# The state group's output matrices on VectorE, and its recurrence over 64 chunks in two levels of eight

## The chip, the cores and the metric

The kernel runs on one core of one Trainium2 chip. The metric is the device time of one execution in microseconds. The kernel before took 1163.69 us in the median of three runs (1162.95 to 1164.85). Five engines work side by side, each through its own queue in order: TensorE (matrix products, PE in the profile), VectorE (DVE), ScalarE (ACT), GpSimd (POOL) and SyncE (SP, which here only issues transfers). SBUF is the on-chip memory, PSUM holds the results of products.

## The reference

One layer of an encoder with a sequence of 256 and a width of 2048, in float32. The projection `x @ w_in` gives q, k, v for 16 attention heads of 64 and u for a state group of width 1024. The change touches the state group alone: 64 groups of 16 channels drive a 64-dimensional complex diagonal state each.

```python
dt = jnp.exp(log_dt)[:, None]
decay = jnp.exp(dt * a_re)
ab_re = decay * jnp.cos(dt * a_im)
ab_im = decay * jnp.sin(dt * a_im)
...
bu_re = jnp.einsum("blgp,gnp->blgn", uf, bb_re)
bu_im = jnp.einsum("blgp,gnp->blgn", uf, bb_im)
...
_, _, s_re, s_im = lax.associative_scan(_complex_linear_combine, elems, axis=1)
y = (jnp.einsum("blgn,gpn->blgp", s_re, c_re)
     - jnp.einsum("blgn,gpn->blgp", s_im, c_im)
     + d_skip * uf)
```

So s[t] = a s[t-1] + B u[t] with complex a, and y = Re(C s) + D u. Then follow a GELU and a gate (`ssm * sigmoid(ssm @ w_glu + b_glu)`), RMS norms of both groups, `w_out`, a layer norm, a feed-forward part with a depthwise convolution (5632 wide), and a second layer norm.

## The kernel before

**The stream of weights.** All large products run over chunks of weights of 128x1024 floats. `dma_chunk` loads one through SyncE's queue, `split_chunk` makes a high part (ScalarE, line 163) and a low part (VectorE, line 164, called lo) out of it, and three products with the two parts take the place of one in float32. In iteration j of `run`, chunk j + 3 is split, chunk j + 7 is loaded and the products of chunk j are issued. Four buffers each hold the raw, high and low parts. Phase 1 has 104 chunks: v (0 to 7), u (8 to 23), v again (24 to 31), k and q in turn (32 to 63, four chunks for a pair of heads), the attention half of w_out (64 to 79), the gate (80 to 87) and the state half of w_out (88 to 103). Phase 2 is the feed-forward part.

**Side work.** At the end of every iteration each generator in `self.sides` whose start has come is advanced by one step: `s5_params` (from chunk 0), `s5_loc` (16), `s5_cm` (22), `s5_kstack` (24), `s5_scan` (35), and the attention of head pair j (from chunk 36 + 4j). `paced` turns a list of instructions with costs into steps: it issues until the summed costs reach a budget, then yields to the next chunk. Small products that come one by one between the large ones go through `put` and `fill`.

**The order of each engine's queue** is not the order of the program alone. A planner takes all instructions with their dependencies, models the engines, and puts on each engine the ready instruction of the highest priority, which is the earliest in the program where nothing else is set (`high_priority` moves some ahead). It also sets the waits. On the chip each engine runs its queue in that fixed order.

**The state group** is computed by chunks of four time steps, 64 chunks in all.
- `s5_params` computes a, its powers and f B on VectorE (tiles in `prm`), 32 columns wide, and `MB`, the matrices a^s f B (line 682, 128x512).
- `s5_loc` transposes MB on TensorE (lt) and multiplies it with u (ll, line 764), which gives every chunk's own contribution to the state, copied into `X[P, 2, 32, 64]`: real and imaginary part, 32 columns (pairs of groups), 64 chunks. `loc_done` is set when that is done.
- `s5_scan` then runs the recurrence over the chunks, `X[c+1] += a^4 X[c]`: 63 steps one after the other, each with four VectorE instructions of 128x64 (lines 819 to 822), with a cost of 1.0 a step and a budget of 2.5 a chunk of weights. `cA` holds the real part of a^4 twice, `cB` the imaginary part with both signs, so that a complex product with a swapped view of X needs two products and two additions.
- `s5_kstack` and `Kt` hold the direct path of u within a chunk (kernels of lags 0 to 3); `Kt` is set to zero by GpSimd (line 866) and filled by eight transfers.
- `s5_cm` forms the output matrices CM = (Re(C a^i), -Im(C a^i)) in four groups of eight columns, in two halves each. Per half GpSimd does two products of 128x512 into scratch (lines 909 and 910, columns 1024 to 2047 of the tile `kcm`) and two additions of 64x512 into CM (line 914), after two memsets per group (lines 900 and 901). The first group lies in half of the tile named `vtok`; the second and third use the slot of MB, the fourth that of `scb`, so they start when MB and scb are no longer read. The second and fourth also wait for `k_done` and `lt_done`.
- `s5_y` multiplies CM with X and Kt with u (line 940), copies the sums to `ysh` (which takes the slot of `kcm`), applies the GELU and splits the result into `ssmhl` (which takes the slot of X) for the gate.

**The attention** of a pair of heads: `evac_k` and `evac_q` add up kz and qt on VectorE (lines 500 and 505), `scores` is a product (S, line 1012), `soft` and `norm` are the softmax on VectorE and ScalarE (lines 1021 to 1031), `trans` transposes the probabilities on TensorE (T, line 1036), `pv` multiplies with v (O, line 1048). There is one kz pair and one qt for all pairs of heads, and the last step of a pair waits for `cm_ready`.

The lines that set the pace of the recurrence:

```python
V.tensor_tensor(u, s[:, ::-1], self.cB, op=ALU.mult)
V.tensor_tensor(w, s, self.cA, op=ALU.mult)
V.tensor_tensor(u, u, t, op=ALU.add)
V.tensor_tensor(t, w, u, op=ALU.add)
yield from self.paced([(1.0, lambda c=c: step(c)) for c in range(63)], 2.5)
```

Of the kernel before, what the change touches and what calls it, by code (L numbers as in the profile page):

```python
# [20 lines left out]
P = 128  # L21
# [36 lines left out]
def host_layout(x, w_in, attn_rel_bias, ssm_a_re, ssm_a_im, ssm_log_dt, ssm_b_re, ssm_b_im,  # L58
# [25 lines left out]

    # groups by (half, column): pairs as they are, and the order whose transposes are pairs
    col, half = np.arange(NP_)[None, :], np.arange(2)[:, None]
# [32 lines left out]
class Builder:  # L119
# [6 lines left out]

# [1 line left out]
    def fill(self):  # L128
# [8 lines left out]

# [1 line left out]
    def add(self, src, mm, post=None, hold=None):  # L139
# [58 lines left out]

# [1 line left out]
    def mm_a(self, ps, hi, lo, xs, k0, first, last, nk=8):  # L200
# [13 lines left out]
    def mm_f(self, ps, hi, lo, k0, first, last, part=None):  # L214
        """product with x1, whose columns are (token tile, high or low part, token)"""
        nc, xs = self.nc, self.x1
        th = lambda a: a.rearrange("p (t h c) -> p t h c", t=2, h=2)[:, :, 0]
        for kk in range(8):
            x = xs[:, k0 + kk]
            w = slice(kk * P, (kk + 1) * P)  # L220
            start, stop = first and kk == 0, last and kk == 7

            def low():
                nc.tensor.matmul(th(ps), lhsT=lo[:, w], rhs=th(x), start=False, stop=False)  # L224
            if part == 0:
                nc.tensor.matmul(ps[:, 0:SEQ], lhsT=hi[:, w], rhs=x[:, 0:SEQ], start=start, stop=False)
                continue
            c = slice(0, 512) if part is None else slice(SEQ, 512)
            if stop:
                low()  # L230
            nc.tensor.matmul(ps[:, c], lhsT=hi[:, w], rhs=x[:, c], start=start and part is None, stop=stop)  # L231
            if not stop:
                low()
# [23 lines left out]

# [1 line left out]
    def build(self):  # L259
# [30 lines left out]

    # phase 1 -----------------------------------------------------------------
    def plan_phase1(self):
# [83 lines left out]
        add_v(1)  # L376
        # k, q
        for j in range(8):
            for c in range(4):
# [9 lines left out]
                self.add(I["wkq"][4 * j + c], mm, post)  # L389
        # w_out, attention half  # L390
        def wo_attn(nb, c):
# [8 lines left out]
        for nb in (2, 3):  # L400
            for c in range(4):
                wo_attn(nb, c)
        # glu
        for f in range(8):
# [3 lines left out]
            self.add(I["wg"][f], mm, lambda f=f: self.evac_glu(f, cur["ps"]))  # L408
        # w_out, state half; the last two blocks one token tile after the other
        for nb in range(4):  # L410
# [53 lines left out]
    def evac_ab(self, ps, name, scale=None):  # L464
        """second half of a product of the split operands, copied out of PSUM"""
        t = self.t1([P, SEQ], name)
# [39 lines left out]

    # S5 ----------------------------------------------------------------------
    def s5_load(self):
# [40 lines left out]
    def s5_params(self):  # L549
# [46 lines left out]
        exp(dec, dec)  # L596
        # sin and cos by the quadrant of th
        ts(k, th, 0.6366197723675814, MUL, MAGIC, ADD)
# [62 lines left out]
        def cmul(o, ia, a, b, w):  # L661
            # o, a: [P, 2, 4, NP_] tiles at index; (o = a*b)
            (orr, oi), (ar, ai), (br, bi) = o, a, b
# [11 lines left out]
        ts(self.scb[:, 1], self.scb[:, 1], -1.0, MUL)  # L675
        # a^(s) f B, s = 0..3
        MB = self.MB = bp.tile([P, 2, NP_, 4, SG], F32, tag="d0", name="MB")
# [23 lines left out]
        cmul(pa(3), None, pa(1), pa(1), None)  # L701
        cA = self.cA = ap.tile([P, 2, NP_], F32, name="cA")
        cB = self.cB = ap.tile([P, 2, NP_], F32, name="cB")
        ops.append((0.2, lambda: V.tensor_copy(cA[:, 0], PA[:, 0, 3])))
        ops.append((0.2, lambda: V.tensor_copy(cA[:, 1], PA[:, 0, 3])))
        ts(cB[:, 0], PA[:, 1, 3], -1.0, MUL)
        ops.append((0.2, lambda: V.tensor_copy(cB[:, 1], PA[:, 1, 3])))
        # -C_im
        ts(self.sc[:, 1], self.sc[:, 1], -1.0, MUL)
# [3 lines left out]
    def reorder(self, a, o):  # L713
        """values of the groups in the order of the transposes, brought to the order of the pairs"""
        nc = self.nc
# [92 lines left out]

    def s5_scan(self):
        while not self.loc_done:  # L810
            yield
        V, X, ap = self.nc.vector, self.X, self.ap_

        def step(c):
            s = X[:, :, :, c]
            t = X[:, :, :, c + 1]
            u = ap.tile([P, 2, NP_], F32, tag="su", bufs=2, name=f"su{c}")
            w = ap.tile([P, 2, NP_], F32, tag="sw", bufs=2, name=f"sw{c}")
            V.tensor_tensor(u, s[:, ::-1], self.cB, op=ALU.mult)
            V.tensor_tensor(w, s, self.cA, op=ALU.mult)  # L820
            V.tensor_tensor(u, u, t, op=ALU.add)
            V.tensor_tensor(t, w, u, op=ALU.add)
        yield from self.paced([(1.0, lambda c=c: step(c)) for c in range(63)], 2.5)
        for _ in range(2):
            yield
        yield from self.s5_y()

    def s5_kstack(self):
# [39 lines left out]
        for g2 in range(2):  # L868
            for i in range(4):
                # rows s >= 3-i hold the kernel of lag s-(3-i)  # L870
                n = SG * (i + 1)
# [5 lines left out]
    def s5_cm(self):  # L877
        nc, bp, ap = self.nc, self.bp, self.ap_
        Gp = nc.gpsimd
        self.CM = []  # L880
# [5 lines left out]
        for pg in range(4):  # L886
# [20 lines left out]
            for ri in range(2):  # L907
                # C holds (re, -im): re(C a) and -im(C a)
                Gp.tensor_tensor(t0, cr if ri == 0 else ci, ar, op=ALU.mult)
                Gp.tensor_tensor(t1, ci if ri == 0 else cr, ai, op=ALU.mult)  # L910
                for g2 in range(2):
                    r = slice(64 * g2, 64 * g2 + 64)
                    o = self.CM[pg][r, ri].rearrange("p c (e g q) -> p g c e q", g=2, q=SG)[:, g2]
                    Gp.tensor_tensor(o, t0[r], t1[r], op=ALU.add if ri == 0 else ALU.subtract)
                yield
# [36 lines left out]
    def evac_glu(self, f, ps):  # L952
# [7 lines left out]
        nc.vector.tensor_tensor(s, ps[:, 0:SEQ], t, op=ALU.add)  # L960
        # sigmoid(z) = (1 + tanh(z / 2)) / 2; the half is taken at the group's norm
        nc.scalar.activation(s, s, AF.Tanh, bias=self.bh[:, f:f + 1], scale=0.5)
# [35 lines left out]

    # attention -----------------------------------------------------------------
    def attention(self, j):  # L1000
# [85 lines left out]

    # w_out and layer norm 1 ------------------------------------------------------
    def load_x(self):
# [81 lines left out]

    # phase 2 -----------------------------------------------------------------
    def plan_phase2(self):
# [176 lines left out]
```

## Time and profile before

| what | value |
|---|---|
| median of three runs | 1163.69 us (1162.95 to 1164.85) |
| span of the profiled execution, first to last instruction | 1161.2 us |
| TensorE busy | 1120.5 us (96%) |
| VectorE busy | 772.8 us (67%) |
| ScalarE busy | 563.1 us (48%) |
| GpSimd busy | 121.6 us (10%) |
| mean granted TensorE clock | 0.985 |

Times in the profile are microseconds from the first instruction of one profiled execution. That execution is listed by its span alone; what lies around it is seen only in the difference to the runs' median. "Busy" is the time in which an engine has an instruction at work; on VectorE one instruction's record can overlap the next one's, so the distance between the starts of two neighbours is what an instruction costs there when many follow each other. Rows of groups give line, engine, operation, output and inputs, shape, the count, busy time, the mean of one in ns, and the idle time before them with what ended it. PEclk is the granted clock of TensorE, 1.00 being full.

### The profile page before, as it was taken

To read this page: it belongs to the slowest core of one execution; us is meant where nothing else is said; L and a number is where in the kernel's file an instruction comes from. 1 tells how busy PE (TensorE), PEld (TensorE's weight loads), DVE (VectorE), ACT (ScalarE), POOL (GpSimd) and SP (SyncE) were. 2 spreads that over 40 slices of the span, in tenths; PEclk is the share of its full clock that TensorE was granted. 3 is DMA by queue.
4 is the path that set the end of the run, shared out by engine and by line. 5 is a ranking of instruction groups with operands and counts; after the bars stand their busy time and mean duration, and the time that the engine had idled before them with its cause. 6 is when DMAs were issued, how large, how long until landed. Compare 5 with 4: busy or idle time off the path is not lost.

```text
span 1161.2 us, 18034 instructions
## 1 busy us (share of the span) xinstructions
PE 1120.5 (96%) x6936; PEld 946.9 (82%) x6936; DVE 772.8 (67%) x1379; ACT 563.1 (48%) x849; POOL 121.6 (10%) x125
## 2 busy tenths in 40 slices
PE   8999959999999889999999999999999999999996
PEld 6887747887787778888888888888888888888885
DVE  7993399994678866666666666666666545454555
ACT  5454325553666545555555555555555433333350
POOL 2031870000001270000000000000000000000001
PEclk9999979999999989999999999999999999999998
DMA  8786324443666446556656666666665766666661
GB/s 299 281 234 147 104 83 146 155 150 97 225 193 204 150 140 212 183 182 189 190 184 183 194 185 182 185 187 190 185 186 190 258 196 192 193 196 192 190 198 73
DMA packets 63589, 212.04 MB, mean 183 GB/s; under 512 B 7568, under 2 KB 13072, under 8 KB 62864
## 3 DMA queue, kind: packets, MB, share of 16 engines
q1 hardware_dynamic: 62320, 208.38, 57.7%
q0 software_dynamic: 896, 2.10, 0.8%
q8 instruction: 54, 0.88, 0.3%
q10 hardware_dynamic: 288, 0.43, 0.1%
q14 instruction: 31, 0.25, 0.1%
HBM read 207.46 MB, written 3.41 MB: 182 GB/s over the span
## 4 chain that ended last, share of the span: by engine, by line
PE 88%; DVE 7%; DMA 2%; POOL 1%; issue 1%; ACT 1%; SPq 0%; ACTq 0%; POOLq 0%; DVEq 0%
PE f L231 27%; PE f L224 14%; PE d L247 7%; PE d L249 7%; PE d L245 7%; PE kq L209 3%; PE u L209 2%; DVE lo L164 2%; PE kq L211 2%; PE oa L245 1%; PE oa L247 1%; PE u L211 1%; PE oa L249 1%; PE glu L209 1%; PE v L247 1%; PE v L249 1%
## 5 line engine op out<-in xcount | busy, mean ns | idle before, releaser
L164 DVE TENSOR_TENSOR lo<-raw,hi 128x1024 fp32r<-128x1024 f32 (+1 forms) x358 | 441.0, 1233 | 246.0 <-ACT hi L163 242.2
L163 ACT CAST hi<-raw 128x1024 fp32r<-128x1024 f32 (+1 forms) x358 | 374.4, 1046 | 299.8 <-PE d L249 125.9
L231 PE MATMUL f<-x1s,hi 128*128 128x512 f32 (+1 forms) x1408 | 491.2, 398 | 6.4 <-ACT hi L163 4.2
L224 PE MATMUL f<-x1s,lo 128*128 128x256 f32 x1408 | 382.6, 283 | 0.5 <-DVE lo L164 0.5
L231 PEld LDWEIGHTS f<-x1s,hi 128*128 128x128 f32 x1408 | 261.2, 190 | 63.1 <-ACT hi L163 4.5
L224 PEld LDWEIGHTS f<-x1s,lo 128*128 128x128 f32 x1408 | 268.0, 190 | 9.5 <-DVE lo L164 1.0
L247 PE MATMUL d<-lo,hid 128*128 128x512 f32 (+1 forms) x360 | 133.4, 371 | 0.0
L245 PE MATMUL d<-hi,hid 128*128 128x512 f32 (+1 forms) x360 | 133.4, 370 | 0.0
L249 PE MATMUL d<-hi,hid 128*128 128x512 f32 (+1 forms) x360 | 133.3, 370 | 0.0
L209 PE MATMUL kq<-xs,hi 128*128 128x512 f32 x240 | 89.8, 412 | 3.1 <-DVE qt L505 3.1
L1324 POOL TENSOR_TENSOR res<-res,gb 128x416 f32<-128x416 f32 x2 | 2.9, 1444 | 721.6 <-ACT res L1323 721.6
L245 PEld LDWEIGHTS d<-hi,hid 128*128 128x128 f32 x360 | 67.8, 188 | 11.8
L247 PEld LDWEIGHTS d<-lo,hid 128*128 128x128 f32 x360 | 67.8, 188 | 11.6
L249 PEld LDWEIGHTS d<-hi,hid 128*128 128x128 f32 x360 | 67.8, 188 | 11.5
L211 PE MATMUL kq<-xs,lo 128*128 128x256 f32 x240 | 69.2, 288 | 0.0
L209 PEld LDWEIGHTS kq<-xs,hi 128*128 128x128 f32 x240 | 45.6, 190 | 14.5 <-DVE qt L505 3.5
L1279 ACT COPY ga<-f 128x256 f32<-128x256 f32 x44 | 16.4, 374 | 82.4 <-PE f L231 82.4
L1286 DVE TENSOR_TENSOR gp<-f,ga 128x256 f32<-128x256 f32 x44 | 18.7, 425 | 45.0 <-ACT ga L1279 45.0
L1279 ACT COPY va<-f 128x256 f32<-128x256 f32 x44 | 16.3, 371 | 64.7 <-PE f L231 64.7
L1298 DVE TENSOR_TENSOR va<-f,va 128x256 f32<-128x256 f32 x44 | 18.7, 424 | 42.3 <-ACT va L1279 42.3
L211 PEld LDWEIGHTS kq<-xs,lo 128*128 128x128 f32 x240 | 45.8, 191 | 0.9
L209 PE MATMUL u<-xs,hi 128*128 128x512 f32 x120 | 43.5, 401 | 0.0
(214 smaller groups left out, 1418.1 us busy)
## 6 DMA issues: line engine op xcount, KB each, us to landing
raw<-wf SPq DMA_DIRECT2D x176, 512.0 KB, 3.7
raw<-wd SPq DMA_DIRECT2D x88, 512.0 KB, 4.3
raw<-wkq SPq DMA_DIRECT2D x32, 512.0 KB, 3.6
raw<-wo SPq DMA_DIRECT2D x32, 512.0 KB, 3.9
raw<-wu SPq DMA_DIRECT2D x16, 512.0 KB, 4.5
raw<-wv SPq DMA_DIRECT2D x15, 512.0 KB, 6.1
raw<-wg SPq DMA_DIRECT2D x8, 512.0 KB, 4.4
bd<-band SPq DMA_DIRECT2D x16, 128.0 KB, 3.0
```

Of the source, the lines that this page charges most:

```text
L163: self.nc.scalar.copy(hi[:, c], raw[:, c])
L164: self.nc.vector.tensor_tensor(lo[:, c], raw[:, c], hi[:, c].bitcast(F32), op=ALU.subtract)
L209: nc.tensor.matmul(ps, start=first and kk == 0, stop=False, **h)
L211: nc.tensor.matmul(ps[:, 0:SEQ], start=False, stop=False, **l)
L224: nc.tensor.matmul(th(ps), lhsT=lo[:, w], rhs=th(x), start=False, stop=False)
L231: nc.tensor.matmul(ps[:, c], lhsT=hi[:, w], rhs=x[:, c], start=start and part is None, stop=stop)
L245: nc.tensor.matmul(ps, lhsT=ah, rhs=wh, start=first and kk == 0, stop=False)
L247: nc.tensor.matmul(ps, lhsT=ah, rhs=wl, start=False, stop=False)
L249: nc.tensor.matmul(ps, lhsT=al, rhs=wh, start=False, stop=last and kk == 1)
L1279: self.nc.scalar.copy(tv, v[:, :, 1])
L1286: nc.vector.tensor_tensor(g[:, 2:].rearrange("p (t c) -> p t c", t=2), p0, t, op=ALU.add)
L1298: nc.vector.tensor_tensor(tv, p0, tv, op=ALU.add)
```

## The change

1. In `s5_cm` the two products and the two additions of each half are issued on VectorE. The memsets stay on GpSimd.
2. `s5_params` no longer forms cA and cB. It forms QR and QI, the powers 1 to 8 of a^4 (real part twice, imaginary part with both signs), by doubling, with 22 small VectorE instructions. QR lies in columns 512 to 1023 of `kcm`.
3. `s5_scan` views the 64 chunks as 8 blocks of 8. First, within all blocks at once, 7 steps of 512 elements (stepping through X by 8 elements); then 7 steps of 64 elements over the last chunks of the blocks; then, block by block, 7 steps of 448 elements that add the power times the last state of the block before. That is 21 steps of four instructions and not 63. Costs are 2.7, 1.1 and 2.4, the budget 3.0 a chunk. Scratch is in the same columns of `kcm` that `s5_cm` uses, and the two empty steps before `s5_y` are gone.

Comments were also taken out.

```diff
@@ s5_params
-        cA = self.cA = ap.tile([P, 2, NP_], F32, name="cA")
-        cB = self.cB = ap.tile([P, 2, NP_], F32, name="cB")
...
+        QR = self.QR = self.kcm[:, 512:1024].rearrange("p (r c k) -> p r c k", r=2, k=8)
+        QI = self.QI = ap.tile([P, 2, NP_, 8], F32, name="QI")
+        q0, q1 = [self.kcm[:, c:c + 128].rearrange("p (c k) -> p c k", k=4) for c in (1024, 1536)]
+        ops.append((0.2, lambda: V.tensor_copy(QR[:, 0, :, 0], PA[:, 0, 3])))
+        ops.append((0.2, lambda: V.tensor_copy(QI[:, 1, :, 0], PA[:, 1, 3])))
+        for n in (1, 2, 4):
+            br, bi = [q.unsqueeze(2).broadcast_to([P, NP_, n]) for q in (QR[:, 0, :, n - 1], QI[:, 1, :, n - 1])]
+            ar, ai = QR[:, 0, :, 0:n], QI[:, 1, :, 0:n]
...
+            tt(QR[:, 0, :, n:2 * n], s0, s1, SUB)
...
+            tt(QI[:, 1, :, n:2 * n], s0, s1, ADD)
+        ops.append((0.3, lambda: V.tensor_copy(QR[:, 1], QR[:, 0])))
+        ops.append((0.3, lambda: V.tensor_scalar(QI[:, 0], QI[:, 1], -1.0, None, op0=ALU.mult)))
@@ s5_scan
-        def step(c):
...
-        yield from self.paced([(1.0, lambda c=c: step(c)) for c in range(63)], 2.5)
-        for _ in range(2):
-            yield
+        X = self.X.rearrange("p r c (b k) -> p r c b k", k=8)
...
+        def madd(cost, o, s, ar, ai, shape):
+            n = math.prod(shape[1:])
+            def f():
+                u, w = (self.kcm[:, c:c + n].rearrange("p (r x) -> p r x", r=2) for c in (1024, 1536))
...
+                V.tensor_tensor(u, s[:, ::-1], ai, op=ALU.mult)
+                V.tensor_tensor(w, s, ar, op=ALU.mult)
+                V.tensor_tensor(u, u, o, op=ALU.add)
+                V.tensor_tensor(o, w, u, op=ALU.add)
+            ops.append((cost, f))
+        sh = [P, 2, NP_, 8]
+        one = lambda q, k: q[:, :, :, k]
+        for k in range(1, 8):
+            bc = lambda q: one(q, 0).unsqueeze(3).broadcast_to(sh)
+            madd(2.7, X[:, :, :, :, k], X[:, :, :, :, k - 1], bc(QR), bc(QI), sh)
+        for b in range(1, 8):
+            madd(1.1, X[:, :, :, b, 7], X[:, :, :, b - 1, 7], one(QR, 7), one(QI, 7), [P, 2, NP_])
+        sh2 = [P, 2, NP_, 7]
+        for b in range(1, 8):
+            madd(2.4, X[:, :, :, b, 0:7], X[:, :, :, b - 1, 7].unsqueeze(3).broadcast_to(sh2),
+                 QR[:, :, :, 0:7], QI[:, :, :, 0:7], sh2)
+        yield from self.paced(ops, 3.0)
@@ s5_cm
-                Gp.tensor_tensor(t0, cr if ri == 0 else ci, ar, op=ALU.mult)
-                Gp.tensor_tensor(t1, ci if ri == 0 else cr, ai, op=ALU.mult)
+                V.tensor_tensor(t0, cr if ri == 0 else ci, ar, op=ALU.mult)
+                V.tensor_tensor(t1, ci if ri == 0 else cr, ai, op=ALU.mult)
...
-                    Gp.tensor_tensor(o, t0[r], t1[r], op=ALU.add if ri == 0 else ALU.subtract)
+                    V.tensor_tensor(o, t0[r], t1[r], op=ALU.add if ri == 0 else ALU.subtract)
```

More of the change, by code (lines that the diff above doesn't have):

```diff
@@ L701, in s5_params @@
         cmul(pa(3), None, pa(1), pa(1), None)
-        cA = self.cA = ap.tile([P, 2, NP_], F32, name="cA")
-        cB = self.cB = ap.tile([P, 2, NP_], F32, name="cB")
[L704 to L707, printed above, removed]
+        QR = self.QR = self.kcm[:, 512:1024].rearrange("p (r c k) -> p r c k", r=2, k=8)
[6 more added lines that the diff above has]
+            ar, ai = QR[:, 0, :, 0:n], QI[:, 1, :, 0:n]
+            s0, s1 = q0[:, :, 0:n], q1[:, :, 0:n]
+            tt(s0, ar, br, MUL)
+            tt(s1, ai, bi, MUL)
+            tt(QR[:, 0, :, n:2 * n], s0, s1, SUB)
+            tt(s0, ar, bi, MUL)
+            tt(s1, ai, br, MUL)
+            tt(QI[:, 1, :, n:2 * n], s0, s1, ADD)
+        ops.append((0.3, lambda: V.tensor_copy(QR[:, 1], QR[:, 0])))
+        ops.append((0.3, lambda: V.tensor_scalar(QI[:, 0], QI[:, 1], -1.0, None, op0=ALU.mult)))
         ts(self.sc[:, 1], self.sc[:, 1], -1.0, MUL)
@@ L811, in s5_scan @@
             yield
-        V, X, ap = self.nc.vector, self.X, self.ap_
-        def step(c):
[L815 to L822, printed above, removed]
-        yield from self.paced([(1.0, lambda c=c: step(c)) for c in range(63)], 2.5)
-        for _ in range(2):
-            yield
+        V = self.nc.vector
+        X = self.X.rearrange("p r c (b k) -> p r c b k", k=8)
+        QR, QI = self.QR, self.QI
+        ops = []
+        def madd(cost, o, s, ar, ai, shape):
+            n = math.prod(shape[1:])
+            def f():
+                u, w = (self.kcm[:, c:c + n].rearrange("p (r x) -> p r x", r=2) for c in (1024, 1536))
+                if len(shape) == 4:
+                    u, w = (t.rearrange("p r (c k) -> p r c k", k=shape[3]) for t in (u, w))
+                V.tensor_tensor(u, s[:, ::-1], ai, op=ALU.mult)
[15 more added lines that the diff above has]
+        yield from self.paced(ops, 3.0)
         yield from self.s5_y()
@@ L878, in s5_cm @@
         nc, bp, ap = self.nc, self.bp, self.ap_
-        Gp = nc.gpsimd
+        Gp, V = nc.gpsimd, nc.vector
         self.CM = []
```

## The prediction

> **What bounds the kernel now.** I read the page first, then busy time by stretch, then the waits of TensorE, and last the single instructions of the stretch that stood out.
>
> ```profile
> span 1161.2 us, 18034 instructions
> PE 1120.5 (96%) x6936; PEld 946.9 (82%) x6936; DVE 772.8 (67%) x1379; ACT 563.1 (48%) x849; POOL 121.6 (10%) x125
> POOL 2031870000001270000000000000000000000001
> PEclk9999979999999989999999999999999999999998
> ```
>
> TensorE is the bound as a whole. Of GpSimd's 121.6 us most lies in the fourth to sixth slice (29 us each), and the granted clock falls exactly behind it. The next rows cut phase 1 at the places where something changes (columns: stretch, its length, busy time and instructions of PE, PEld, DVE, ACT, POOL, then the clock).
>
> ```profile
> 80.00:114.00 34.00, 33.56 (x366) 26.56 (x365) 12.86 (x14) 16.18 (x23) 8.29 (x12) 1.00 0.68 166
> 114.00:142.60 28.60, 28.60 (x222) 20.98 (x221) 11.18 (x12) 8.62 (x12) 25.40 (x21) 1.00 0.36 112
> 149.70:167.25 17.55, 5.47 (x31) 2.92 (x31) 17.45 (x24) 4.81 (x14) 16.39 (x13) 0.61 0.27 81
> 203.00:259.30 56.30, 56.12 (x322) 46.23 (x324) 55.71 (x230) 30.65 (x72) 2.96 (x4) 1.00 0.48 150
> ```
>
> From 114 to 142.6 TensorE is full while VectorE idles 28.6 - 11.2 = 17.4 us. From 149.7 to 167.25 TensorE works 5.5 of 17.6 us, at a clock of 0.61, and VectorE is full. From 203 to 259 both are full. What TensorE waited for between 143 and 180:
>
> ```profile
> PE T L1036 <- DVE sT L1031: 8.4, 2, 6.3
> PE kq L209 <- DVE qt L505: 3.1, 1, 3.1
> PE O L1048 <- ACT pT L1040: 0.6, 1, 0.6
> ```
>
> That is 12.1 us. Behind the long wait the matmuls also ran slowly for a time:
>
> ```profile
> 157.51 1.11 PE L1048 MATMUL O<-pT,vtok 128*64 128x256 f32 x2 [0.57 <-ACT pT L1040]
> ...
> 170.62 0.44 PE L209 MATMUL kq<-xs,hi 128*128 128x512 f32 x1
> ```
>
> The first takes 1.11 us where the same product later takes 0.58 (quoted below), and at 170.6 the pace is normal again. From 156.0 to 170.6 there are 14.6 - 5.8 (the shorter waits) = 8.8 us of work at half speed, which would take 4.4 less. So at most 12.1 + 4.4 = 16.5 us is to be had here. Why VectorE was late shows in its own times, the first five rows from 146.3 to 167 and the last five the same kinds from 168 to 258.
>
> ```profile
> L164 DVE TENSOR_TENSOR lo<-raw,hi 128x1024 fp32r<-128x1024 f32 x2 | 4.2, 2120 | 0.0
> L819 DVE TENSOR_TENSOR su<-X,cB 128x64 f32<-128x64 f32 x3 | 3.6, 1185 | 0.1
> L822 DVE TENSOR_TENSOR X<-sw,su 128x64 f32<-128x64 f32 x3 | 3.2, 1077 | 0.1
> L1031 DVE TENSOR_SCALAR sT<-sT,mx 128x256 f32<-128x256 f32 x2 | 2.7, 1346 | 0.0
> L1031 DVE TENSOR_SCALAR sT<-sT,mx 128x128 f32<-128x128 f32 x2 | 2.7, 1332 | 0.0
> ...
> L164 DVE TENSOR_TENSOR lo<-raw,hi 128x1024 fp32r<-128x1024 f32 x22 | 27.5, 1249 | 0.0
> L822 DVE TENSOR_TENSOR X<-sw,su 128x64 f32<-128x64 f32 x57 | 15.2, 267 | 0.3
> L819 DVE TENSOR_TENSOR su<-X,cB 128x64 f32<-128x64 f32 x56 | 15.1, 269 | 0.5
> L1031 DVE TENSOR_SCALAR sT<-sT,mx 128x256 f32<-128x256 f32 x11 | 3.8, 347 | 0.0
> L1031 DVE TENSOR_SCALAR sT<-sT,mx 128x128 f32<-128x128 f32 x11 | 3.1, 280 | 0.0
> ```
>
> Each costs 0.8 to 1.05 us more: 2 x 0.87 + 3 x 0.92 + 3 x 0.81 + 2 x 1.00 + 2 x 1.05 = 11.0 us on these twelve. In that time GpSimd forms the output matrices, and the ends fall together:
>
> ```profile
> 151.16 2.08 POOL L910 TENSOR_TENSOR kcm<-prm 128x512 f32<-128x512 f32 x1
> 152.28 0.99 DVE L1022 TENSOR_SCALAR mx<-mx 128x2 f32<-128x2 f32 x1
> ```
>
> A VectorE instruction over two elements ends at 153.27, with GpSimd's (153.24). So the two engines hold each other up, and the stall is VectorE's backlog. By 203 it is gone, and from there TensorE sets the pace.
>
> **The change part by part.** **The output matrices:** 16 instructions of 128x512 and 16 of 64x512 go from GpSimd to VectorE; GpSimd keeps eight memsets and that of Kt. Prices on VectorE come from these rows (instructions of one group follow each other at the distance of their starts):
>
> ```profile
> 71.16 0.68 DVE L682 TENSOR_TENSOR MB<-MB,mbt 128x512 f32<-128x512 f32 x1
> 71.76 0.68 DVE L682 TENSOR_TENSOR MB<-prm 128x512 f32<-128x512 f32 x1
> 76.40 1.25 DVE L563 TENSOR_TENSOR prm<-prm 128x32 f32<-128x32 f32 x11
> 145.86 0.26 DVE L820 TENSOR_TENSOR sw<-X,cA 128x64 f32<-128x64 f32 x1
> 146.04 0.26 DVE L821 TENSOR_TENSOR su<-su,X 128x64 f32<-128x64 f32 x1
> ```
>
> 512 elements in a row cost 0.60, so 32 instructions cost 19.2 us. The first group's eight (4.8 us) can start when the parameters are done near 80, where VectorE idles 21 us up to 114. The other 24 (14.4 us) must wait until the slots of MB and scb come free behind the kernel-stack product:
>
> ```profile
> 109.52 3.92 PE ks L839 x128
> ```
>
> From 113.4 on they fit the 17.4 us that are idle before 142.6. I count them at nothing. The cover is thin: whatever spills past 142.6 is paid, up to 9.6 us for two groups. The gain is that the contention is gone: 11 us of VectorE's time.
>
> **The powers QR, QI:** 22 small instructions for 4 removed, between 0.11 (the 32-element row) and 0.26 us each, 2.4 to 5.7 us, say 3.8, near 80, where the idle time just named follows. Nothing.
>
> **The recurrence:** 63 steps x 4 instructions of 64 elements become 7 x 4 of 512, 7 x 4 of 64 and 7 x 4 of 448. Unmixed, a step takes 0.97 us, from one first instruction to the next:
>
> ```profile
> 143.74 0.26 DVE L819 TENSOR_TENSOR su<-X,cB 128x64 f32<-128x64 f32 x1
> ...
> 144.71 0.27 DVE L819 TENSOR_TENSOR su<-X,cB 128x64 f32<-128x64 f32 x1
> ```
>
> Mixed with other work the gaps between dependent instructions are filled, and it costs 4 x 0.18 = 0.72; I take 0.75. From 168 to 258 VectorE did 57 steps (43 us) and the rest of 22 chunks (rows above: 22 splits), with no idle time, so the rest is (90 - 43) / 22 = **2.15 us a chunk**. The new first level walks X in steps of 8 elements, which no row shows at 512. Lower bound: 0.60 each as in MB, 2.4 us a multiply-add. Upper: 32 elements in a row start 0.107 apart, 512 start 0.60 apart, so 64 in a row would be 0.14, but the strided rows show 0.18; 0.04 over 64 elements is 0.32 over 512, hence 0.92 each, and 4.1 with gaps where an instruction needs the one before. I take three at 0.92 and the last, which only writes strided, at 0.7, with 0.15 of gaps: **3.6 us**, since the recurrence's own walk is the nearest row. Second level: a step as now, 0.75 to 0.97, take 0.80. Third: runs of 7 in a row, 0.53 to 0.6 each, take 2.3. Sum 7 x 3.6 + 7 x 0.8 + 7 x 2.3 = 25.2 + 5.6 + 16.1 = **46.9 us** (37 to 52), against 63 x 0.75 = 47 now. The two levels save VectorE nothing; they only hand the work out faster, over 14 chunks where 25 were used (cost units 2.7, 1.1, 2.4 against a budget of 3.0, and 63 x 1.0 against 2.5).
>
> [...]
>
> **What it does to TensorE:** the recurrence starts at 143.74, with the split of chunk 41 just done. Splits run up to three chunks ahead of the products. The last of the new recurrence is emitted with chunk 52, so ahead of the split of chunk 56. VectorE reaches that split after 15 chunks of other work: 143.7 + 46.9 + 15 x 2.15 = **222.8**. Before, chunk 40 starts behind the last wait:
>
> ```profile
> 167.25 0.79 PE L209 MATMUL kq<-xs,hi 128*128 128x512 f32 x1 [3.07 <-DVE qt L505]
> 207.22 0.58 PE O L1048 x2
> 222.37 0.58 PE O L1048 x2
> ```
>
> Four chunks take 15.15 us (the two rows are the same product of successive head pairs), 3.8 each, so chunk 56 starts at 167.25 + 16 x 3.8 = 228.0. Without any stall TensorE would be there at 228.0 - 16.5 = 211.5, but it can't pass the split. Gain 228.0 - 222.8 = **5.2 us**. From there on TensorE is the bound as before, VectorE has 1.7 us a chunk to spare, and the y products, the same number as now, stand among the kq products and not behind them. Scratch in kcm, and ysh in its slot, add only orders on VectorE itself. The results ysh and ssmhl come earlier than now, so nothing behind them waits longer. The profiled span of 1161.2 becomes 1156.0; the median of 1163.69 lies 2.5 us above the span (start and end outside it), so the forecast is **1158.5**.
>
> [...]
>
> **The rivals.**
> *Clean:* the first level costs near 2.4 us, VectorE then reaches the split at 143.7 + 37 + 32.2 = 212.9, almost where TensorE is; gain 15.1, 1148.6. For it: MB's products read broadcast operands at 0.68. Against it: the strided rows.
> *Even:* the first level costs 4.1 and the rest its upper bounds, 143.7 + 52.3 + 32.2 = 228.2; gain 0, 1163.7.
> *Slower:* TensorE is held by the transposes and not by the splits. It runs in order, and a transpose waits for the softmax, which stands in VectorE's queue among instructions of 0.92 instead of 0.18 us.
>
> ```profile
> 183.41 0.33 PE L1036 MATMUL T<-ident,sT 128*128 128x128 f32 x1 [0.79 <-DVE sT L1031]
> 198.09 0.30 PE L1036 MATMUL T<-ident,sT 128*128 128x128 f32 x1 [0.20 <-DVE sT L1031]
> 203.13 1.21 DVE L164 TENSOR_TENSOR lo<-raw,hi 128x1024 fp32r<-128x1024 f32 x1
> ```
>
> At 203.13 VectorE splits chunk 52 while TensorE, by 3.8 us a chunk, stands in 49.4: the transposes, not the splits, held it 2.6 chunks back. If that lead can't be used up, TensorE is at 53.4 when VectorE reaches 56 at 222.8; before, it was there at 167.25 + 13.4 x 3.8 = 218.2. Loss 4.6 us, 1168.3. It decides from a lead of 1.4 chunks that stays unused. Against it: the order of TensorE's queue is planned anew with the longer instructions, so transposes can stand later.
>
> **How the numbers follow.** Forecast, a gain of 2.3 to 10 us: 0.40. Clean: 0.18. Even, within 2.3 us (0.2%, about what a measurement of this kernel tells from no change): 0.18. Slower: 0.24. So faster 0.58, same 0.18, slower 0.24. The range reaches from the clean case with a little over (1147) to the slower one (1168.5); the forecast's own is 1153 to 1161.
>
> **What would show it.** Right: VectorE's splits stay near 1.25 us and the softmax's scaling near 0.35 from 146 to 167; GpSimd shows no 512-element products; the 6.3 us wait shrinks below 3; VectorE is full from 143 to about 223 and TensorE shows small waits there; y products start near 225, among the kq products. The strided first level shows at 0.9 to 1.0 us an instruction (0.68 if clean). Wrong: output-matrix instructions on VectorE behind 143.7; waits on sT that together pass 16.5 us; a new wait of y for X; a change outside 80 to 300 us.

## The result and the profile after

The changed kernel takes 1171.32 us (median of 4 runs, 1170.06 to 1171.85) against 1164.27 us (1162.95 to 1165.29) for the kernel before on the same chip: a ratio of 1.0061, 95% interval 1.0048 to 1.0073. It is slower by 7 us. The forecast was 1158.5 us. The profiled execution has a span of 1169.5 us against 1161.2.

The head of the page, the kernel after:

```profile
span 1169.5 us, 17878 instructions
PE 1122.2 (96%) x6936; PEld 949.3 (81%) x6936; DVE 788.0 (67%) x1261; ACT 565.8 (48%) x850; POOL 81.0 (7%) x93
POOL 2031100000002180000000000000000000000001
PEclk9999988999999998999999999999999999999998
```

GpSimd's block in the fifth and sixth slice is gone (121.6 us before, 81.0 now) and the dip of the granted clock is less deep, but two slices long (146 to 205 us) and not one. The same four stretches as before the change (length, busy time and instructions of PE, PEld, DVE, ACT, POOL, then the clock, DMA share and GB/s):

```profile
80.00:114.00 34.00, 33.56 (x365) 26.56 (x364) 23.42 (x42) 16.35 (x23) 5.64 (x10) 1.00 0.64 170
114.00:142.60 28.60, 27.93 (x235) 21.62 (x234) 24.78 (x33) 9.03 (x12) 8.62 (x7) 1.00 0.38 113
149.70:167.25 17.55, 15.63 (x73) 12.19 (x74) 16.93 (x31) 5.33 (x14) 0.00 (x0) 0.81 0.31 89
203.00:259.30 56.30, 49.05 (x939) 40.78 (x939) 39.35 (x95) 25.10 (x51) 1.53 (x2) 0.94 0.38 115
```

The stall of 149.7 to 167.25 has gone: TensorE works 15.6 us there, not 5.5. The last row shows where the time went instead. Before, TensorE was full from 203 to 259 (56.1 us at a clock of 1.00). Now it is idle for 7.3 us of it, and the clock is 0.94. TensorE's waits from 130 to 320 us, the longest kinds first (us in total, times, longest):

```profile
PE T L1065 <- DVE sT L1060: 6.4, 2, 3.6
PE kq L209 <- DVE kz L500: 3.9, 2, 2.2
PE y L969 <- issue: 3.1, 1, 3.1
PE O L1077 <- ACT pT L1069: 1.9, 3, 0.7
PE oa L245 <- ACT pa L1139: 1.7, 1, 1.7
PE S L1041 <- DVE qt L505: 1.1, 1, 1.1
PE y L969 <- DVE ysh L970: 1.0, 1, 1.0
```

The wait on the scaled scores sT is down from 9.6 us in this stretch to 6.4. Waits on k (kz), on q (qt), on pa (a result of the attention half of w_out), and a wait within y that names no releaser ("issue"), have come in. No wait of this stretch names a split (lo), in this kernel or in the one before. VectorE's groups from 130 to 270 us:

```profile
L164 DVE TENSOR_TENSOR lo<-raw,hi 128x1024 fp32r<-128x1024 f32 x27 | 33.0, 1221 | 8.7 <-ACT hi L163 8.6
L838 DVE TENSOR_TENSOR kcm<-X,QI 128x512 f32<-128x512 f32 x7 | 8.1, 1161 | 0.0
...
L841 DVE TENSOR_TENSOR X<-kcm 128x512 f32<-128x512 f32 x7 | 8.0, 1149 | 0.0
...
L841 DVE TENSOR_TENSOR X<-kcm 128x448 f32<-128x448 f32 x7 | 4.3, 618 | 0.0
...
L1060 DVE TENSOR_SCALAR sT<-sT,mx 128x256 f32<-128x256 f32 x12 | 4.2, 348 | 0.2
...
L943 DVE TENSOR_TENSOR CM<-kcm 64x512 f32<-64x512 f32 x4 | 2.7, 685 | 0.1
```

Splits (1.22 us) and scalings (0.35) are undisturbed. Level 1 takes 1.15 us an instruction, level 3 0.62. The last row is the fourth group of output matrices. Its eight instructions run between recurrence steps, since they share scratch with them.

One more view is needed for the rest. The table counts ScalarE's copies of weight chunks (hi, L163) from 0 and gives when the n-th starts, in us behind the first experiment (the kernel before with only the output matrices moved to VectorE). It is worked out from the timelines of ScalarE. Copy n is of chunk n - 1, since chunk 0 is copied on another line and chunks 1 and 2 in two halves each. In the changed kernel the recurrence lies between copies 40 and 57; in the kernel before it goes on to 256.8 us. Nearly all products y lie between 56 and 84 in all of them.

```
copy   before  after | neighbours  late y  both  y in halves | spread
  36     -0.1   -0.3 |       +0.1    -0.1  -0.1         +0.4 |   -0.1
  44     +6.4   +2.2 |       -0.6    +2.4  -0.9         +2.9 |   +1.1
  48    +16.8   +5.1 |       -0.7    +5.9  -0.9         +5.5 |   +7.3
  56    +16.9  +15.3 |       +3.6   +16.4  +3.3        +15.7 |   +5.1
  84    +17.1  +25.3 |      +12.0   +19.5  +5.9        +19.1 |  +11.2
 200    +18.1  +26.4 |      +12.4   +18.8  +6.9        +19.4 |  +12.5
```

The first two columns tell most of the result. At copy 56 the changed kernel is 1.6 us ahead of the kernel before. By copy 84 it is 8.2 us behind. The kernel before loses 0.2 us between the two, the changed one 10.0. Behind copy 84 nothing more changes between the two.

### The profile page after: what moved, and what is told of

Read it like the earlier page. It is cut to its first block, busy times and chain, and to the rows that moved or that the text cites. A ratio compares the mean times of both kernels' runs of the same rounds, so it can differ in the third digit from the quotient of the medians.

```text
span 1169.5 us, 17878 instructions
## 1 busy us (share of the span) xinstructions
PE 1122.2 (96%) x6936; PEld 949.3 (81%) x6936; DVE 788.0 (67%) x1261; ACT 565.8 (48%) x850; POOL 81.0 (7%) x93
## 4 chain that ended last, share of the span: by engine, by line
PE 86%; DVE 8%; issue 2%; DMA 2%; POOL 1%; ACT 1%; SPq 0%; ACTq 0%; POOLq 0%; DVEq 0%
PE f L231 27%; PE f L224 14%; PE d L245 7%; PE d L247 7%; PE d L249 7%; PE u L209 2%; PE kq L209 2%; DVE lo L164 2%; PE oa L245 1%; PE kq L211 1%; PE oa L249 1%; PE oa L247 1%; PE u L211 1%; PE glu L209 1%; PE v L247 1%
## 5 line engine op out<-in xcount | busy, mean ns | idle before, releaser
L163 ACT CAST hi<-raw 128x1024 fp32r<-128x1024 f32 (+1 forms) x358 | 374.5, 1047 | 309.1 <-PE d L249 125.5
```

The lines of the kernel that those rows point to most:

```text
L163: self.nc.scalar.copy(hi[:, c], raw[:, c])
```

## The experiments

All times are medians on one chip for each group of runs. The kernel before took 1163.3 to 1163.7 us beside them, and 1164.27 beside the changed kernel, so a difference between an experiment and the changed kernel's 1171.32 is good to about 1 us.

**1. Only the output matrices on VectorE.** The kernel before, with four lines of the change:

```diff
-                Gp.tensor_tensor(t0, cr if ri == 0 else ci, ar, op=ALU.mult)
+                nc.vector.tensor_tensor(t0, cr if ri == 0 else ci, ar, op=ALU.mult)
...
-                    Gp.tensor_tensor(o, t0[r], t1[r], op=ALU.add if ri == 0 else ALU.subtract)
+                    nc.vector.tensor_tensor(o, t0[r], t1[r], op=ALU.add if ri == 0 else ALU.subtract)
```

> The first part alone: the output matrices on VectorE, the recurrence in 63 steps as before. Contention theory (GpSimd's products held VectorE up by 11 us between 146 and 167, and that was TensorE's stall): the 6.3 us wait on sT shrinks below 3 us, VectorE's splits there take 1.25 us instead of 2.12, and the time falls by 6 to 12 us, to 1152 to 1158. Rival (the 19 us of products on VectorE are what made the changed kernel slow): 1168 or more. If the spilled part of the products eats what the contention gave: 1162 to 1166.

Measured: 1146.09 us, ratio 0.9857 (0.9838 to 0.9876), span 1143.1. Its waits from 130 to 320 us are all that is left of the stall:

```profile
PE T L1036 <- DVE sT L1031: 2.1, 4, 1.3
PE O L1048 <- ACT pT L1040: 1.8, 2, 1.2
PE y L940 <- DVE ysh L941: 1.3, 3, 0.5
```

So this part alone gains 17.2 us, more than the 6 to 12 expected, and everything that is lost is lost by the second part.

**2. Only the new recurrence.** The changed kernel with the output matrices on GpSimd:

```diff
-                V.tensor_tensor(t0, cr if ri == 0 else ci, ar, op=ALU.mult)
+                Gp.tensor_tensor(t0, cr if ri == 0 else ci, ar, op=ALU.mult)
...
```

> The second part alone: the two-level recurrence, the output matrices on GpSimd as before. Price theory (the first level's steps of 8 elements cost 1.15 us an instruction and not 0.6 to 0.9): slower than before by more than the changed kernel, since the contention stays as well and strikes longer instructions, 1172 to 1182. Rival (the recurrence is harmless, the matrices on VectorE are the loss): 1158 to 1164.

Measured: 1185.95 us, ratio 1.0199 (1.0182 to 1.0216), 22.6 us slower than before and above the range of the price theory. The waits of TensorE, and level 1 on VectorE (110 to 270 us; the last field is the idle time before it):

```profile
PE T L1065 <- DVE sT L1060: 15.3, 5, 4.1
PE S L1041 <- DVE qt L505: 5.6, 3, 3.5
PE y L969 <- issue: 4.2, 4, 1.6
```

```profile
L838 DVE TENSOR_TENSOR kcm<-X,QI 128x512 f32<-128x512 f32 x7 | 8.1, 1156 | 6.2 <-POOL CM L943 6.2
```

The contention stays (at 145.0 us a VectorE instruction over two elements takes 1.08 us, where those of the changed kernel take 0.16), and the shared scratch kcm now makes VectorE wait 6.2 us for GpSimd. The recurrence costs 22.6 us beside the old matrices and 1171.3 - 1146.1 = 25.2 us beside the new ones. The parts don't help each other.

**3. Level 1 on neighbours.** The changed kernel, walking level 1 over runs of eight neighbouring chunks. It adds the wrong chunks, so its states are not the layer's, while instructions and sizes stay:

```diff
-            madd(2.7, X[:, :, :, :, k], X[:, :, :, :, k - 1], bc(QR), bc(QI), sh)
+            madd(2.7, X[:, :, :, k], X[:, :, :, k - 1], bc(QR), bc(QI), sh)
```

> The changed kernel with the first level walking runs of 8 neighbours in place of steps of 8; it adds up the wrong chunks in that level, so the state's values are not those of the reference, while every instruction keeps its size. Price theory: the first level falls from 1.15 to 0.69 us an instruction, 28 x 0.46 = 13 us less on VectorE, and the time falls by 7 to 12 us, to 1159 to 1164. Density theory (the recurrence is handed out over too few chunks whatever it costs): 1167 or more. Bunch theory (the y products in one bunch starve TensorE of instructions): the gap of 3.1 us without a named releaser and the half clock behind it stay, so no more than 7 us fall away.

Measured: 1156.85 us, ratio 0.9945 (0.9930 to 0.9960). 14.4 of the 25.2 us come back. The same instruction of level 1, in the same view:

```profile
L838 DVE TENSOR_TENSOR kcm<-X,QI 128x512 f32<-128x512 f32 x7 | 4.8, 686 | 0.0
```

It takes 0.69 where the strided one takes 1.16 us. Over 28 instructions that is 13 us, nearly the gain. In the table ("neighbours") the lag at copy 56 falls from 15.3 to 3.6, but from 56 to 84 it still grows by 8.4. The wait within y stays (3.0 us in two), as the bunch theory said, yet twice the 7 us that it allowed came back.

**4. One multiply-add a chunk.**

```diff
-        yield from self.paced(ops, 3.0)
+        yield from self.paced(ops, 1.75)
```

> The changed kernel with a budget of 1.75 instead of 3.0 a chunk, so that the recurrence is handed out over 25 chunks as before. Density theory: VectorE keeps up, TensorE's waits on kz, qt and sT between 167 and 215 (8 us) go, 1160 to 1165. Price theory: the first level is still 31 us in 11 chunks, 2.8 us a chunk on top of 2.15 against 3.8, so a part of the waits stays, 1164 to 1169. Bunch theory: the y products start later, and the gap stays only if they are still in one bunch.

Measured: 1166.87 us, ratio 1.0034 (1.0017 to 1.0051), 4.4 us below the changed kernel. Each level-1 step still costs its chunk about 4.4 us of VectorE, so the lag at copy 56, counted as in the table, is no smaller (17.7). With a budget of 3.0 level 1 already took six chunks, so the edit spreads mainly the two later levels. A wait of 5.0 us on k came in. What went is most of the wait within y (0.8 us in all), and y now ran from 238 us and not from 217. This asked for experiment 5.

**5. y 14 chunks later.**

```diff
         yield from self.paced(ops, 3.0)
+        for _ in range(14):
+            yield
         yield from self.s5_y()
```

> The changed kernel with the outputs y starting 14 chunks later (53 us at 3.8 us a chunk), about where the kernel before has them; nothing else is moved. Theory that VectorE's load in the recurrence costs most: only the 3.1 us gap inside y and the slow clock behind it (0.67 over 10 us, 3.3 us) can go, so 1165 to 1169 against the changed kernel's 1171.3. Rival, that the bunching of y among the last softmaxes is what costs: y then meets nothing, and the time falls by 8 us or more, to 1163 or less. A third: y is needed by then and the gate waits for it, 1172 or more.

Measured: 1164.94 us, ratio 1.0014 (1.0005 to 1.0024), 6.4 us below the changed kernel. This is the lower edge of the first theory's range and 2 us above the rival's. What came back is as much as that theory gave the gap and the slow clock behind it (3.1 and 3.3 us), though the wait on pa (1.7 us at 311) is gone too. In the table ("late y") copy 56 is as late as in the changed kernel, and only 3.1 us are lost behind it. Two stretches that hold y, first of the changed kernel, then of this one:

```profile
217.00:245.00 28.00, 23.28 (x785) 19.49 (x787) 16.81 (x46) 9.35 (x25) 0.75 (x1) 0.88 0.36 104
```

```profile
260.00:300.00 40.00, 38.98 (x824) 30.12 (x823) 18.24 (x37) 17.45 (x30) 0.74 (x1) 1.00 0.31 99
```

TensorE idles 4.7 us and runs at 0.88 in the one; it idles 1.0 us at full clock in the other.

**6. The output matrices all ahead of the recurrence.**

```diff
-                yield
+                if ri == 1 and pg in (0, 2):
+                    yield
             self.cm_ready = pg + 1
```

> The changed kernel with the output matrices written in one piece per two groups, so that all of them stand in VectorE's queue ahead of the recurrence and nothing of them waits there for the shared scratch. Theory that VectorE's load in 143 to 170 us sets the waits: the eight instructions found behind recurrence steps (4.9 us) go into the idle time before, and 4 to 6 us come back: 1165 to 1168. Rival, that they were filling time in which the engine would have waited anyway: 1170 to 1172.

Measured: 1170.22 us, ratio 1.0055 (1.0037 to 1.0073). The interval covers the changed kernel's ratio, so the rival held: the fourth group behind recurrence steps (4.9 us of VectorE by their starts) cost at most about 1 us.

**7. The recurrence laid out by the instruction, at measured prices.** On top of 6, each instruction is an item of its own:

```diff
-            madd(2.7, X[:, :, :, :, k], ...)
+            madd(1.1, X[:, :, :, :, k], ...)
-            madd(1.1, X[:, :, :, b, 7], ...)
+            madd(0.2, X[:, :, :, b, 7], ...)
-            madd(2.4, X[:, :, :, b, 0:7], ...)
+            madd(0.53, X[:, :, :, b, 0:7], ...)
-        yield from self.paced(ops, 3.0)
+        yield from self.paced(ops, 1.6)
```

> As the kernel with the output matrices early, and the recurrence is laid out by the instruction at measured prices (1.1, 0.2 and 0.53 us) with 1.6 us of it a chunk, over 32 chunks in place of 14.5. A chunk on VectorE is then 2.15 + 1.6 = 3.75 us against TensorE's 3.8. Theory that what costs is the load per chunk and not its sum: nearly all waits of TensorE on the scores and q go, and the time comes within 4 us of the kernel with the output matrices on VectorE alone (1146.1), 1146 to 1150, strided operands and all. Rival, that the strided sum (57 us of recurrence against 45) has to be paid wherever it lies: 1156 to 1162. Rival, that y is late by it (last y near 285 us): 1150 to 1156 with a wait of the gate or of y on X.

**8. The same, on neighbours** (0.6 in place of 1.1, and 1.5 a chunk; again the wrong chunks are added):

> As the spread kernel, with level 1 on runs of eight neighbours (the wrong chunks are added; as many instructions and elements) at 0.6 us each, 37 us in 25 chunks at 1.5. By the load theory 2.15 + 1.5 = 3.65 us a chunk: no waits on the scores, 1145 to 1148, the same as the spread kernel or up to 2 us below. By the rival of the sum it stands 8 to 14 us below the spread kernel.

Measured: 1155.52 us (ratio 0.9931, 0.9915 to 0.9948) with strides and 1157.04 us (0.9939, 0.9921 to 0.9956) with neighbours. Both miss their first theories. The time of experiment 7 lies where its rivals put it, but by neither's reason. No product waits for X or the gate, and laid out thinly the strided walk costs no more than the neighbours. So what counts in this layout is VectorE's load per chunk and not the sum of the recurrence, and yet neither comes to 1146. Of the 15 us that experiment 7 lies below 6, some may be y's: y now begins at 268 us, and experiment 5 gained 6.4 by moving y alone. Each keeps one long wait near the first softmaxes, and a gap in y. The longest rows of 130 to 320 us, strided first, then neighbours:

```profile
PE T L1062 <- DVE sT L1057: 5.1, 2, 4.3
PE y L966 <- issue: 2.0, 1, 2.0
```

```profile
PE kq L209 <- DVE kz L500: 5.3, 1, 5.3
PE y L966 <- issue: 1.9, 3, 0.9
```

**9. The price of the stride by itself.** Level 1's seven steps at four distances (the wrong chunks are added in all but the last; one run, 1162.25 us, read for its single instructions):

```diff
+            d = (0, 1, 1, 2, 2, 4, 4, 8)[k]
+            Y = self.X[:, :, :, 0:8 * d].rearrange("p r c (b k) -> p r c b k", k=d)
+            o, i = (X[:, :, :, k], X[:, :, :, k - 1]) if d == 1 else (Y[:, :, :, :, d - 1], Y[:, :, :, :, d - 2])
-            madd(2.7, X[:, :, :, :, k], X[:, :, :, :, k - 1], bc(QR), bc(QI), sh)
+            madd(2.7, o, i, bc(QR), bc(QI), sh)
```

> The changed kernel with the seven steps of level 1 walking chunks 1, 1, 2, 2, 4, 4 and 8 apart (4, 8, 16 and 32 bytes; wrong chunks are added for all but the last; as many instructions and elements). [...] Rival, a price that grows with the distance: four levels, about 0.68, 0.75, 0.9, 1.15. Rival, that every distance but 4 bytes costs the full price: 0.68, then 1.1 throughout.

VectorE's timeline, the first product of a step at 4, 8, 16 and 32 bytes (start, duration):

```profile
131.88 0.68 DVE L838 TENSOR_TENSOR kcm<-X,QI 128x512 f32<-128x512 f32 x1
...
146.91 0.68 DVE L838 TENSOR_TENSOR kcm<-X,QI 128x512 f32<-128x512 f32 x1
...
159.46 1.07 DVE L838 TENSOR_TENSOR kcm<-X,QI 128x512 f32<-128x512 f32 x1
...
169.67 1.16 DVE L838 TENSOR_TENSOR kcm<-X,QI 128x512 f32<-128x512 f32 x1
```

Two prices and not four: 0.68 at 4 and 8 bytes, 1.07 to 1.16 at 16 and 32. The two rivals fall. It makes no difference whether the strided operand is read (L838) or written (L841: 0.68 and 1.04 at 8 and 16 bytes). Against the rows at 4 and 8 bytes the step costs 0.4 to 0.5 us on 512 elements. Why it lies between 8 and 16 bytes no run shows.

**10. The first experiment with the matrices in one piece** (the edit of 6 in the kernel of 1):

> The kernel before with the output matrices on VectorE, in one piece per two groups, so that none of them lies between the first recurrence steps; the recurrence is the old one. The spread kernels differ from this one in the recurrence alone. If the early order of the matrices had a price, some of the 10 us between the spread kernels and the kernel with the output matrices alone (1146.1) shows here: 1149 to 1156. If not, 1143 to 1147.

Measured: 1146.56 us, ratio 0.9850 (0.9836 to 0.9865), the same as experiment 1. The 9 us by which experiment 7 stands above it are the recurrence's and its y's.

**11. The spread recurrence six chunks later, and 12. its level 1 in halves of 16 pairs:**

```diff
+        for _ in range(6):
+            yield
         yield from self.paced(ops, 1.6)
```

```diff
-        sh = [P, 2, NP_, 8]
+        sh = [P, 2, NP_ // 2, 8]
...
-            madd(1.1, X[:, :, :, :, k], X[:, :, :, :, k - 1], bc(QR), bc(QI), sh)
+            for h in range(2):
+                c = slice(16 * h, 16 * h + 16)
+                bc = lambda q: one(q, 0)[:, :, c].unsqueeze(3).broadcast_to(sh)
+                madd(0.55, X[:, :, c, :, k], X[:, :, c, :, k - 1], bc(QR), bc(QI), sh)
```

> The spread kernel with its recurrence starting six chunks (some 23 us) later. Theory that the remaining 10 us come from the pile at 138 to 152 us, where the first steps meet the first softmaxes and three splits in a row: the 4.3 us wait on the scores goes with its slow clock, 1148 to 1152, if y (from 290 us) isn't late. Rival, that the grain of 1.1 us an instruction makes some wait wherever the recurrence lies: one long wait (3 us or more) at another place and 1154 to 1158. Rival, y late: a wait of the gate, 1158 or more.

> The spread kernel with each instruction of level 1 cut into two of 16 pairs (256 elements, 0.55 us each): the same start, the same sum, half the grain. Theory of the grain, that a softmax or k step finds whole 1.1 us instructions ahead of it in VectorE's queue: the long wait shrinks under 2 us, 1147 to 1151. Theory of the pile at the start: as the spread kernel, 1154 to 1158, with a wait of 3 to 5 us at 140 to 155 us.

Measured: 1153.87 us (ratio 0.9913, 0.9897 to 0.9930) for the later start, 1159.45 us (0.9962, 0.9947 to 0.9976) for the halves. The later start gains 1.7 us, short of its theory. The halves lose 3.9: the theory of the grain falls. The pile's wait is there (3.6 us from 147 us), but the time lies above its range too. TensorE's longest waits in the halves:

```profile
PE kq L209 <- DVE kz L500: 4.5, 2, 3.4
PE T L1064 <- DVE sT L1059: 3.6, 1, 3.6
```

They are waits of the same kinds, at 147 and 170 us, in another order of VectorE's queue. What places such a wait was not found. It stays open, at 9 us at most.

**13. Neighbours and late y together** (the edits of 3 and 5):

> The changed kernel with both edits that gave time back one by one: level 1 on runs of eight neighbours (wrong chunks are added; 14.4 us alone) and the outputs y 14 chunks later (6.4 us alone). If these are two separate losses they add up: 1171.3 - 20.8 = 1150.5, 1149 to 1152, so that at most some 4 us of the 25 between the changed kernel and the one with the output matrices alone (1146.1) stay unnamed. Rival, that the two are one loss seen twice (a late VectorE that pushes the last scores into y): 1154 to 1157, as with the neighbours alone.

Measured: 1151.93 us, ratio 0.9902 (0.9887 to 0.9917). Alone the two give 14.4 and 6.4 us, together 19.4 of the 20.8. So they are separate losses, and 1151.9 - 1146.1 = 5.8 us of the new recurrence's 25.2 are left. The trace shows most of them: from 130 to 320 us TensorE idles 8.1 us against 5.2 in experiment 1 (waits on sT, pT, kz and qt), and it runs at a clock of 0.50 for 3.4 us, which costs half of that.

**14. y in halves:** one `yield` after each half of a quarter of y, so that y starts where it did but half as many small products follow one another.

```diff
                 nc.vector.tensor_copy(ysh[:, 2 * pg + f]...)
-            yield
+                yield
```

> The changed kernel with each quarter of y cut in two, so that 96 small products and not 192 follow one another between large ones, and y takes eight chunks from the same start. Theory that a long run of small products starves TensorE of instructions wherever it lies: the 3.1 us gap goes with its slow clock and the time comes to the late y's, 1164 to 1167. Rival, that the place is what matters (the last scores and loads of that stretch): the gap stays at 2 us or more, 1169 to 1172.

Measured: 1165.31 us, ratio 1.0019 (1.0010 to 1.0029), 6.0 us below the changed kernel and the same as the late y. So the gap went without y being moved. The order of TensorE's instructions shows what experiments 5 and 14 have in common. In the changed kernel 560 of y's 768 small products follow one another from 217.5 to 236.1 us with no product of a weight chunk between them. The longest such run is 184 in the kernel before, 132 in experiment 5 and 272 here. The runs of 560 and more in experiments 2, 3, 6 and 9 hold such stops too (the longest 1.7, 2.2, 1.8 and 2.8 us). The changed kernel's TensorE at the gap, with the stretches of 5 us around it, and then two stretches of this kernel:

```profile
227.15 0.24 PE L969 MATMUL y<-up,Kt 128*32 128x64 f32 x3
230.45 0.64 PE L969 MATMUL y<-X,CM 128*32 128x63 f32 x14 [3.06 <-issue]
```

```profile
225.00:230.00 5.00, 2.31 (x148) 2.01 (x137) 1.62 (x2) 0.00 (x0) 0.00 (x0) 0.98 0.75 222
230.00:235.00 5.00, 4.55 (x114) 3.67 (x114) 0.61 (x1) 0.00 (x0) 0.00 (x0) 0.50 0.02 7
```

```profile
220.00:225.00 5.00, 3.98 (x161) 3.24 (x161) 5.00 (x14) 1.47 (x5) 0.00 (x0) 1.00 0.75 217
225.00:230.00 5.00, 5.00 (x61) 4.27 (x63) 3.98 (x20) 2.77 (x11) 0.00 (x0) 1.00 0.83 280
```

In the changed kernel TensorE stops for 3.06 us amid y with no engine to wait for, and behind that the clock is 0.50 for 5 us. In this kernel weights load just as hard (a DMA share of 0.75 and 0.83). From 220 to 225 its small products idle 0.98 us for ysh and no more than 0.16 without a releaser; from 225 to 230 mainly larger products follow, and TensorE is full. What the changed kernel's DMA queues moved from 224 to 232 us (packets, MB, share of 16 engines):

```profile
q1 hardware_dynamic: 383, 1.37, 55.8%
q8 instruction: 2, 0.03, 1.8%
```

In that time two packets of instructions came in, of 16 KB each, in the microseconds from 227 and from 231. The first falls near the start of the gap, behind a weight chunk of 512 KB. That a long run of small products uses up instructions faster than they are brought in, as the expectations of experiments 3 and 14 suppose, was not shown: the trace doesn't say whose instructions a packet holds. Nor is length the whole condition: experiment 7 stops for 1.96 us in a run of 96.

## Why the prediction was wrong, step by step

**The contention: right.** At most 16.5 us were to be had; experiment 1 gained 17.2, a little over. VectorE's splits and scalings are back to 1.21 and 0.35 us from 146 to 167 us, as was to be seen. One reading was too strong: 51.5 of GpSimd's 121.6 us lie in the fourth to sixth slice, not most of them.

**The output matrices at nothing: right.** VectorE is busy 23.4 and 24.8 us in the two stretches ahead of 142.6, and TensorE works 33.56 and 27.93 us in them as against 33.56 and 28.60. One group of four spilled, through the shared scratch. The prediction named that as a sign of being wrong, but it cost no more than a microsecond (experiment 6). "Only orders on VectorE itself" held for the kernel as it is. With the matrices on GpSimd the same scratch cost 6.2 us of VectorE's time (experiment 2).

**The powers at nothing: right**, by the same two stretches.

**Level 1: mis-sized.** 0.92 us an instruction was the upper bound; it measured 1.15, and by starts 1.05 to 1.1. That is 4.2 to 4.4 us a multiply-add, where 3.6 was taken and 4.1 was the ceiling. By starts the level took 29.6 us in all and not 25.2; the second took 5.7 (5.6 in the sum) and the third 15.4 (16.1). The step that failed is the scaling up of the 64-element rows: their 0.04 us, times eight, gave 0.32 on 512 elements, while the stride costs 0.4 to 0.5 (experiment 9). Whether a short instruction hides a part of it no run shows. Nor is a bound worked out from a difference of two small numbers a bound.

**The split of chunk 56 as TensorE's limit, and the gain of 5.2 us: the mechanism failed.** VectorE began that split at 224.7 us, near the 222.8 of the sum, but by luck: the recurrence began at 131.94 and not at the 143.74 carried over from the kernel before, and three more chunks of other work, the spilled matrices and the dearer level 1 used that lead up. TensorE was not standing at the split. In the kernel before it began chunk 56 at 229.1, 10.5 us behind the split (218.6). In experiment 5, with nearly all of y out of the way, it began it at 232.1, 8.1 us behind the split (224.0). So the lead of the splits was never used up, and in place of a gain of 5.2 us there was a loss of 3.0. What held TensorE were results that stand in VectorE's queue between the splits. Against experiment 1 the waits on sT grew from 2.1 to 6.4 us, and waits on k and q (3.9 and 1.8) came in. ScalarE, which copies ahead, shows a gain of 1.6 us at copy 56 and none at copy 57, chunk 56's own (216.9 us before, 217.1 after).

**y at nothing: the other step that failed.** "The y products, the same number as now, stand among the kq products and not behind them" was true of the number, but 560 of them stood in one run. The changed kernel loses 10.0 us between copies 56 and 84, and the kernel before 0.2. Some 6 us of it are the run of small products, with its gap of 3.06 us and the slow clock behind it (experiments 5 and 14). The rest are the last wait on k (1.70 us at 214.1), those on ysh, and the wait on pa (1.72 us at 311).

**The rival "slower"** gave 1168.3, near the result. Its mechanism, a TensorE held by what VectorE's queue delivers late and not by the splits, with a lead that stays unused, is the one that experiment 5 shows, with 3.0 us of loss at chunk 56 where it had 4.6. But it named the transposes alone, and it knew nothing of y's 6 us, so that its number came so near is partly luck.

**The clock: put at nothing, and it cost some 10 us.** The sum has no term for a slow clock behind the waits that come back. In the changed kernel, with waits of 2.80, 2.20 and 3.64 us (they end at 150.4, 172.0 and 182.9) and with the gap of 3.06 came four stretches at a clock of 0.50:

```profile
151.30:158.10 6.80, 5.93 (x17) 3.80 (x18) 6.74 (x13) 1.62 (x5) 0.00 (x0) 0.50 0.43 140
171.80:175.10 3.30, 3.15 (x10) 2.69 (x11) 3.27 (x5) 0.00 (x0) 0.00 (x0) 0.50 0.02 5
182.00:188.80 6.80, 5.18 (x16) 3.69 (x17) 6.80 (x25) 1.35 (x5) 0.00 (x0) 0.50 0.47 125
229.80:236.60 6.80, 6.15 (x119) 5.01 (x120) 1.23 (x2) 0.41 (x1) 0.00 (x0) 0.50 0.03 10
```

That is 20.4 us of work at half the clock, an estimated 10.2 us lost. In experiment 1, with no wait over 1.3 us, the clock is 1.00 from 130 to 320 us. TensorE idles 20.4 us there in the changed kernel and 5.2 in experiment 1. The difference of 15.2 and the 10.2 come to 25.4 us, about all that the new recurrence cost (25.2). So on top of the waits came two thirds as much again at the slow clock.

## What to carry to other kernels

Ask of a two-level scheme what distance it walks, and price it by a row of the same length and the same distance: on VectorE 8 bytes between fp32 elements cost nothing here (0.68 us for 512 elements, as at 4), and 16 cost some 60% more (1.07). Before you call one result the limit, look in the old trace at how far ahead of its use it is made. Where an engine has a certain load per chunk to spare, lay moved work out by its measured price, one instruction at a time. The same recurrence at the same sum was 15 us faster when spread, a part of which may be y's later place. Work that is "only earlier" need not be free: here a run of 560 small products without large ones between lost 6 us, so look at what moved work will follow and precede. And of a change in two parts, time each alone: here one gave 17 us and the other took 25, and the best kernel found is the first part by itself, at 1146 us.

## What the runs showed of the hardware that was not expected

- At the four distances measured, the price of a stride is a step and not a slope: 0.68 us at 4 and 8 bytes, 1.07 to 1.16 at 16 and 32, for 512 fp32 elements a partition, read or written.
- TensorE stopped for 2 to 3 us with no engine to wait for, amid small products (3.06 us in the changed kernel, in a run of 560 with a DMA share of 0.75; 1.96 us in experiment 7, in a run of 96). With the stop in the changed kernel came 6.8 us at a clock of 0.50.
- With waits of 2.2 to 3.6 us came stretches of 3.4 to 6.8 us at a clock of 0.50 (changed kernel).
- Cutting VectorE's instructions in two did not shorten TensorE's waiting: on k and sT it was 8.1 us in all against 5.6, though the longest wait fell from 4.3 to 3.6 (experiments 12 and 7).
